# Four edits to a hybrid attention encoder: a joined product in band attention, later loads in the down projection, and a ring and two places around the output norms

## The chip, the core and the metric

The kernel runs on one core of a Trainium2 chip. The core has TensorE (PE in the profile, with its weight loads as PEld), VectorE (DVE), ScalarE (ACT), GpSimd (POOL) and SyncE (SP), which here issues the DMA transfers in the order of the program. Each engine has its own list of instructions in one order; semaphores tie the lists together. The metric is the device time of one execution in microseconds, lower is better.

## The reference, cut to what matters

One layer of an encoder, for a prompt of 2048 tokens and a sample of 32 tokens with 128 cached positions, width 1024, everything in float32:

```
z = rmsnorm(x) @ w_in                     # 1024 x 3072: q, k, v of two groups
oa = differential attention (4 heads, two maps of 64, values of 128), chunk-causal
ob = band attention (8 heads of 64), a 64-token chunk sees itself and 8 chunks before
     p = softmax(q k / 8 + bias, masked);  ob = p @ v
h  = x + concat(rmsnorm(oa), rmsnorm(ob)) @ w_out
h  = h + square(relu(rmsnorm(h) @ w_up)) @ w_down          # 4096 wide
h  = h + sigmoid(h @ w_ple_gate) * (p_in @ w_ple_proj)
y  = rmsnorm(h)                            # and the new keys and values are outputs
```

## The kernel before

Precision. The operands of the matmuls are in a reduced float32 form (fp32r in the profile's rows), so each operand is split in two: `hi`, a rounded copy (made on ACT or DVE), and `lo`, the rest (made on DVE or POOL). A product is then three matmuls: hi·hi, hi·lo, lo·hi. `mm3` (L254 and on) issues them, and `split` makes the parts.

Blocks. The tokens lie in four blocks of 512, 544, 512 and 512 columns (the sample rides in block 1). Tensors between the stages go through DRAM: `qS`, `kS`, `vS` (projections), `oT` (attention output), `hS` (the residual stream), `uS` (the MLP's hidden layer for blocks 2 and 3).

Stages. Norm and input projection per block (`prep`, `proj`); differential attention for the first half (`attn_a`); band attention (`attn_b`) for pairs of 128-token query tiles, interleaved with projections of later blocks and later with the output projection and the MLP of block 0; the output norm's sums (`onorm`), then `oload` (reads `oT`, scales, splits) and `outproj`; the MLP of blocks 0 and 1 by blocks (`mlp_up`, `mlp_down`); for blocks 2 and 3 together a seven-product scheme on half-size matrices (`uphase`, then `dphase`); the gates (`gate`, `gatepair`); the final norm.

Who sets the order. The Python code weaves generators into one another (`weave`, `weave2`), and the tile framework's scheduler then sets each engine's order by a simulated time line. A tile belongs to a ring of `bufs` buffers under a tag; a tile that is written again waits for the readers of the buffer's last content.

Band attention of one head and one pair of query tiles (`attn_b_pair`). Scores come in `sb` (PE), bias and row maximum on DVE, exponent and scaling on ACT. The weights are transposed on PE (`tpb`) and split: hi parts into `pH` (ACT), lo parts into `pL` (DVE), both tiles of six key tiles by 256 queries. Then per key tile two matmuls with the same stationary tile `vt` add into one PSUM tile `o` of 256 columns: one moves `pH`, one `pL`. The stationary tile has 128 columns: 64 of v's hi part, 64 of its lo part, so rows 0 to 63 of `o` hold v-hi times the weights and rows 64 to 127 v-lo times the weights. Where a key tile serves one query tile alone, the matmul has 128 columns. Last, ACT copies rows 64 to 127 to `t1`, and DVE adds rows 0 to 63. `o` has one buffer.

The down projection of blocks 2 and 3 (`dphase`). Seven products (numbers m = 3, 5, 7, 4, 2, 6, 1 in this order), each of eight steps c, each step of two k. For each k one `dx` (from `ut`, read from `uS`) and one `dw` (from one or two `wd`, read from `w_down`) are split, then 4 x 3 matmuls of 512 columns go to four PSUM tiles `dp`. `dx` has four buffers. At a product's end DVE adds `dp` into tiles of `h` (L1249). Product 3 adds into block 3 alone, product 5 into both blocks. Beside this PE works on the gates of blocks 0 and 1 (`gps`, `pps`), whose weights share the raw buffers with `ut`.

The ties (`hstep`, L1699). `h` of blocks 2 and 3 is read back from `hS` in 16 transfers of 256 KB. To keep them from starting early, each destination first gets one column copied from a `dx`; the transfer then has to wait for that copy.

Output projection. `oload(1)` is woven with `outproj(0)`, and the norm of block 0 (`norms(0)`, which runs `cnorm`) with `outproj(1)`. All take their scratch from the tag `tmp` of the pool `wk`, three buffers. `weave2(..., ONP)` places the steps of the output norms of blocks 0 and 1 between the steps of the last projections.

Of the kernel before, what the change touches and what calls it, by code (L numbers as in the profile page):

```python
# [12 lines left out]
F32 = mybir.dt.float32  # L13
F32R = mybir.dt.float32r
AF = mybir.ActivationFunctionType
ALU = mybir.AluOpType
# [3 lines left out]
P = 128  # L20
# [24 lines left out]
HALVES = [(0, 1), (2, 3)]  # L45
# [68 lines left out]
OW = 1  # L114
# [1 line left out]
JA0 = [(0, 1), (2, 3, 8)]  # L116
JA1 = [(4, 5), (6, 7)]
JB = [(0, 1), (2, 3, 8), (4, 5), (6, 7)]
ONP = (16, 1, 6)
ONQ = (8, 1, 1)  # L120
PW = 256
GL = 3
# [20 lines left out]
def weave(main, side, step, i=0, n=1):  # L143
    for _ in main:
        if i % step == 0:
            for _ in range(n):
                next(side, None)
        i += 1
    drain(side)
# [47 lines left out]
class Kern:  # L197
# [554 lines left out]
    def attn_b_pair(self, h, j, kt, v, kb, bb, q, ahead, pool, ps_s, ps_t, ps_o):  # L752
        nc = self.nc
# [4 lines left out]
        else:  # L758
            tiles, t0, nq = [2 * j, 2 * j + 1], tcol(256 * j), 256
        kfirst = 0 if samp else max(0, 2 * j - 4)  # L760
        pH = pool.tile([P, 6, 256], F32R, tag="pH", bufs=2, name="pHb")
        pL = pool.tile([P, 6, 256], F32R, tag="pL", bufs=2, name="pLb")
        spans = []
        for qi, t in enumerate(tiles):
            if samp:
# [30 lines left out]
            for x0 in range(0, len(kts), 4):  # L796
                ch = kts[x0 : x0 + 4]
                tp = ps_t.tile([P, 4, P], F32, tag="tp", name="tpb")
                for x, (i, kn) in enumerate(ch):
                    nc.tensor.transpose(  # L800
                        tp[:kn, x, :nr], e[:, P * (x0 + x) : P * (x0 + x) + kn], self.ident[:nr, :nr]
                    )
                groups = [(0, len(ch), P)] if not samp else [(0, 1, P), (1, 1, SS)]
                for a0, na, kn in groups:
                    sl = ch[0][0] - kfirst + a0
                    h_ = pH[:kn, sl : sl + na, P * qi : P * qi + nr]
                    l_ = pL[:kn, sl : sl + na, P * qi : P * qi + nr]
                    s_ = tp[:kn, a0 : a0 + na, :nr]
                    nc.scalar.activation(h_, s_, AF.Copy)
                    nc.vector.tensor_tensor(l_, s_, h_.bitcast(F32), op=ALU.subtract)  # L810
        ahead()
        o = ps_o.tile([P, 256], F32, tag="o", name="ob")
        order = []
        if samp:
            order = [(0, P, 0, nq), (1, SS, 0, nq)]
# [6 lines left out]
            order += [(i, P, 128, 256) for i in s1 if i not in s0]  # L822
        for x, (i, kn, qa, qb) in enumerate(order):
            vt = v[:kn, (SP - kb) // P + i] if samp else v[:kn, i - kb // P]
            for y, pt in enumerate((pH, pL)):
                nc.tensor.matmul(
                    o[:, qa:qb], vt, pt[:kn, i - kfirst, qa:qb],
                    start=x == 0 and y == 0, stop=x == len(order) - 1 and y == 1,
                )
        t1 = pool.tile([64, 256], F32, tag="t1", bufs=2, name="t1")[:, :nq]  # L830
        nc.scalar.activation(t1, o[64:128, :nq], AF.Copy)
        nc.vector.tensor_tensor(t1, o[0:64, :nq], t1, op=ALU.add)
        self.dma(self.oT[64 * m : 64 * m + 64, gi, t0 : t0 + nq], t1)

    def raw_o(self, wk, k, t0, n):
# [360 lines left out]
    def dphase(self, h, pool, md, step):  # L1196
# [32 lines left out]
        for m, sq, so, outs in plan:  # L1229
            ps = [md.tile([P, 512], F32, tag="mm", name="dp") for _ in range(4)]  # L1230
            for c in range(8):
                for k, (w, x) in enumerate(operands(m, sq, so, c)):
                    if m == 3 and k == 0:
                        step(c, x)
                    for d in range(4):
                        sl = slice(P * d, P * d + P)
                        self.mm3(
                            ps[d], [(w[:, 0, sl], w[:, 1, sl], x[:, 0], x[:, 1])],
                            start=c + k == 0, stop=c == 7 and k == 1,
                        )  # L1240
                if c < 7:
                    yield
            adds = [(d, q, op) for d in range(4) for q, op in outs]
            if m == 1:
                adds.sort(key=lambda x: x[1])
            for d, q, op in adds:
                i, t = int(q[0]) - 1, int(q[1]) - 1
                hv = h[2 + t][4 * i + d]
                nc.vector.tensor_tensor(hv, hv, ps[d], op=op)  # L1249
            yield  # L1250
# [231 lines left out]
    def run(self):  # L1482
        tc, nc, a = self.tc, self.nc, self.a
        with ExitStack() as top:
# [118 lines left out]
            def norms(b, act, ps):  # L1603
                r = self.colnorm(acc[b][0], b, 1.0 / D, wk, ps, "mm", None)
                yield
                yield from self.cnorm(b, wk, act, cn, r)

            acc = {b: [] for b in range(4)}
            with ExitStack() as x:
                oq = Sized(opened(x, "oq", 2), BLK, True)  # L1610
                weave(self.outproj(0, wk, oa[0], mm, acc[0]), self.oload(1, wk, oq, oa), 1, 0, OW)
                weave(self.outproj(1, wk, oa[1], mm, acc[1]), norms(0, actq, mm), 1, 1)
            hq = opened(sq_, "hq", 1)
            uq = Sized(opened(sq_, "uq", 10), BLK)
# [81 lines left out]
            h = {b: hh.tile([P, 8, 512], F32, tag="h", name="h") for b in HALVES[1]}  # L1696
            h = {b: [t[:, d] for d in range(8)] for b, t in h.items()}

            def hstep(c, x):  # L1699
                for b in HALVES[1] if c < 4 else ():  # L1700
                    for d in (2 * c, 2 * c + 1):
                        nc.gpsimd.tensor_copy(h[b][d][:, :1], x[:, 0, :1].bitcast(F32))
                    hmove(b, h[b], True, range(2 * c, 2 * c + 2))

            fk = opened(top, "fk", 1)
            udx, gqx = ExitStack(), ExitStack()
# [90 lines left out]
```

## Time and profile before

| | |
|---|---|
| median of 3 executions | 2965.36 us (2957.69 to 2965.66) |
| profiled execution | 2963.89 us |
| its span, first to last instruction | 2962.1 us |
| mean granted clock of TensorE | 0.993 |
| PE busy | 2899.6 us, 98% of the span |
| DVE, ACT, POOL busy | 1754.8, 1753.6, 1349.1 us |
| DMA | 578 MB, 195 GB/s on average |

A row of a group reads: line, engine, operation, tile written <- tiles read, shape, count | busy us, mean ns of one | idle time before it and what ended it. Durations of matmuls overlap, so the step between two starts tells what one costs. A row of the waits reads: who waited on whom: us in total, times, longest. A row of the time line reads: start us, us, engine, line, operation. A row of the windows gives the stretch, then the busy time and count of each engine, the granted clock, the DMA share and GB/s.

### The profile page before, as it was taken

The page shows a single profiled execution, that of the slowest core. Times are in us where ns is not written, and L with a number is a line of the kernel's source. Part 1 is how long each engine was busy: PE and PEld are TensorE (multiplying, and loading weights), DVE is VectorE, ACT ScalarE, POOL GpSimd, SP SyncE. Part 2 cuts the span into 40 slices and gives each one's busy share as a digit, 9 for nine tenths or more (in the row PEclk, how much of TensorE's full clock was granted, in tenths as well). Part 3 has the DMA queues.
Part 4 walks back from the last instruction along what each step waited for, and adds up shares of the span by engine and source line. Part 5 has one row for each costly group of instructions (what it writes and reads, how often), then busy time and mean ns, then how long its engine had stood idle before and what let it go on. Part 6 is the DMA issues. An engine that isn't in the chain of part 4 may idle for free.

```text
span 2962.1 us, 49251 instructions
## 1 busy us (share of the span) xinstructions
PE 2899.6 (98%) x17041; PEld 2560.4 (86%) x17041; DVE 1754.8 (59%) x3930; ACT 1753.6 (59%) x3729; POOL 1349.1 (46%) x1863
## 2 busy tenths in 40 slices
PE   8999999999999999999999999999999989999998
PEld 7899888998889888888899999889788868888886
DVE  6566664444565543565766564447665656766965
ACT  5566666665666665766777675443545445555554
POOL 4675664333355555655455455440855533133000
PEclk9999999999999999999999999999999999999999
DMA  9975578766677544544743433566443495756811
GB/s 347 328 249 198 192 259 271 219 210 207 226 252 225 192 159 157 166 154 151 240 138 123 148 109 120 183 205 199 164 149 139 146 342 191 267 194 202 265 64 57
DMA packets 299785, 578.28 MB, mean 195 GB/s; under 512 B 34672, under 2 KB 132080, under 8 KB 299536
## 3 DMA queue, kind: packets, MB, share of 16 engines
q1 hardware_dynamic: 299536, 575.13, 58.3%
q8 instruction: 135, 2.21, 0.3%
q14 instruction: 114, 0.93, 0.1%
HBM read 443.81 MB, written 131.22 MB: 194 GB/s over the span
## 4 chain that ended last, share of the span: by engine, by line
PE 89%; DMA 5%; DVE 3%; ACT 2%; issue 1%; POOL 1%; SPq 0%; ACTq 0%; DVEq 0%; POOLq 0%
PE s L607 4%; PE ups L269 4%; PE ups L267 4%; PE ups L268 4%; PE dps L267 4%; PE dps L268 4%; PE dps L269 4%; PE qps L267 4%; PE qps L269 4%; PE qps L268 4%; PE xps L269 3%; PE xps L268 3%; PE xps L267 3%; PE dp L267 3%; PE dp L269 3%; PE dp L268 3%
## 5 line engine op out<-in xcount | busy, mean ns | idle before, releaser
L230 POOL TENSOR_TENSOR wl<-wr,wh 128x256 fp32r<-128x256 f32 x888 | 667.8, 783 | 703.2 <-ACT wh L235 583.2
L235 ACT ACTIVATE wh<-wr 128x1024 fp32r<-128x1024 f32 x258 | 272.5, 1056 | 214.4 <-PE dps L268 43.5
L267 PE MATMUL ups<-cH,wh 128*128 128x272 f32 (+1 forms) x768 | 249.9, 326 | 2.3 <-ACT cH L235 1.2
L267 PE MATMUL dps<-uh,wh 128*128 128x272 f32 (+1 forms) x768 | 250.5, 328 | 1.5 <-DVE h L1001 1.1
L269 PE MATMUL ups<-cH,wl 128*128 128x272 f32 (+1 forms) x768 | 249.7, 326 | 0.6 <-DVE wl L241 0.6
L268 PE MATMUL ups<-cL,wh 128*128 128x272 f32 (+1 forms) x768 | 249.6, 325 | 0.0
L268 PE MATMUL dps<-ul,wh 128*128 128x272 f32 (+1 forms) x768 | 248.7, 324 | 0.2 <-DVE ul L241 0.2
L269 PE MATMUL dps<-uh,wl 128*128 128x272 f32 (+1 forms) x768 | 247.9, 324 | 0.0
L267 PE MATMUL qps<-aH,wh 128*128 128x512 f32 (+3 forms) x640 | 228.8, 357 | 6.6 <-DVE qk L487 3.0
L269 PE MATMUL qps<-aH,wl 128*128 128x512 f32 (+3 forms) x640 | 227.4, 355 | 0.0
L268 PE MATMUL qps<-aL,wh 128*128 128x512 f32 (+3 forms) x640 | 226.8, 354 | 0.0
L268 PE MATMUL dp<-dx,dw 128*128 128x512 f32 x448 | 177.9, 397 | 0.0
L267 PE MATMUL dp<-dx,dw 128*128 128x512 f32 x448 | 168.1, 399 | 9.1 <-ACT dx L235 9.1
L269 PE MATMUL dp<-dx,dw 128*128 128x512 f32 x448 | 174.9, 397 | 0.0
L607 PE MATMUL s<-ka,q 128*128 128x512 f32 (+3 forms) x640 | 173.3, 368 | 0.5 <-DVE nm L616 0.4
L788 DVE CUSTOM_DVE_ANT_0 eb<-sb,bb 128x320 f32<-128x320 f32 (+2 forms) x232 | 104.1, 478 | 109.3 <-PE tpb L800 105.0
L613 DVE TENSOR_REDUCE nm<-s 128x1 f32<-128x512 f32 (+1 forms) x192 | 122.1, 641 | 77.8 <-PE s L607 76.0
L267 PEld LDWEIGHTS ups<-cH,wh 128*128 128x128 f32 x768 | 145.2, 189 | 15.2 <-ACT cH L235 1.5
L267 PEld LDWEIGHTS dps<-uh,wh 128*128 128x128 f32 x768 | 144.6, 189 | 14.0 <-DVE h L1001 2.6
L269 PEld LDWEIGHTS ups<-cH,wl 128*128 128x128 f32 x768 | 145.0, 189 | 11.9 <-DVE wl L241 1.0
L268 PEld LDWEIGHTS ups<-cL,wh 128*128 128x128 f32 x768 | 145.3, 189 | 11.6 <-DVE cL L241 0.4
L268 PEld LDWEIGHTS dps<-ul,wh 128*128 128x128 f32 x768 | 144.8, 189 | 10.6 <-DVE ul L241 0.4
(278 smaller groups left out, 8949.4 us busy)
## 6 DMA issues: line engine op xcount, KB each, us to landing
wd<-w_down SPq DMA_DIRECT2D x96, 512.0 KB, 5.2
q<-qS SPq DMA_DIRECT2D x128, 256.0 KB, 4.2
v<-vSa SPq DMA_DIRECT2D x64, 512.0 KB, 3.6
wr<-w_up SPq DMA_DIRECT2D x64, 512.0 KB, 3.8
wr<-w_down SPq DMA_DIRECT2D x64, 512.0 KB, 3.8
ut<-uS SPq DMA_DIRECT2D x56, 512.0 KB, 4.3
wr<-w_qk SPq DMA_DIRECT2D x54, 512.0 KB, 5.2
kS<-qk SPq DMA_DIRECT2D x32, 512.0 KB, 5.4
```

Of the source, the lines that this page charges most:

```text
L230: nc.gpsimd.tensor_tensor(out[:, sl], a[:, sl], b[:, sl], op=op)
L235: nc.scalar.activation(hi, raw, AF.Copy)
L267: nc.tensor.matmul(ps, lh, rh, start=start and i == 0, stop=False)
L268: nc.tensor.matmul(ps, lh, rl, start=False, stop=False)
L269: nc.tensor.matmul(ps, ll, rh, start=False, stop=stop and i == n - 1)
L607: nc.tensor.matmul(s, q[:, m, hl, P * qi : P * qi + nr], kt[:, m, k0 - kb : k0 - kb + n], start=hl == 0, stop=hl == 1)
L613: nc.vector.tensor_reduce(nmx, s, axis=AX.X, op=ALU.max, negate=True)
L788: nc.vector.tensor_tensor_reduce(e[:, w * i : w * i + w], s, bb[:nr, b0 + w * i : b0 + w * i + w], 1.0, -3e38, ALU.add, ALU.max, st[:, 3 + ...
```

## The change

Four edits.

1. Band attention's two tiles `pH` and `pL` become one tile `pHL` with the parts side by side, and one matmul per key tile moves both: 2 x 256 columns, or 2 x 128 where a key tile serves one query tile. `o` has 512 columns in two halves, the product with the hi parts and that with the lo parts. At the end DVE adds rows 0 to 63 of both halves, one after the other; ACT copies rows 64 to 127 of the first half alone, so v-lo times the lo weights is left out of the sum now.
2. `hstep` is called in every product. The loads of block 3 are tied to steps 4 to 7 of product 3 (two each), those of block 2 to steps 0 to 7 of product 5 (one each). The tying copy is on ACT instead of POOL.
3. `oload(1)` and `cnorm` of block 0 take their scratch from a ring of their own, `ot`, of two buffers. As the pool is then a `Mix`, `oload` reads one tile ahead.
4. The output norms of blocks 0 and 1 move: their two steps stood at 16 and 22 (block 0) and 17 and 23 (block 1) of the projection's steps, and stand at 17 and 24, and at 23 and 30.

```
-ONP = (16, 1, 6)
+ONP = (17, 6, 7)
...
-        pH = pool.tile([P, 6, 256], F32R, tag="pH", bufs=2, name="pHb")
-        pL = pool.tile([P, 6, 256], F32R, tag="pL", bufs=2, name="pLb")
+        pHL = pool.tile([P, 6, 2, 256], F32R, tag="pHL", bufs=2, name="pHLb")
...
-                    h_ = pH[:kn, sl : sl + na, P * qi : P * qi + nr]
-                    l_ = pL[:kn, sl : sl + na, P * qi : P * qi + nr]
+                    h_ = pHL[:kn, sl : sl + na, 0, P * qi : P * qi + nr]
+                    l_ = pHL[:kn, sl : sl + na, 1, P * qi : P * qi + nr]
...
-        o = ps_o.tile([P, 256], F32, tag="o", name="ob")
+        o = ps_o.tile([P, 2, 256], F32, tag="o", name="ob")
...
-            for y, pt in enumerate((pH, pL)):
-                nc.tensor.matmul(
-                    o[:, qa:qb], vt, pt[:kn, i - kfirst, qa:qb],
-                    start=x == 0 and y == 0, stop=x == len(order) - 1 and y == 1,
-                )
+            nc.tensor.matmul(
+                o[:, :, qa:qb], vt, pHL[:kn, i - kfirst, :, qa:qb], start=x == 0, stop=x == len(order) - 1
+            )
         t1 = pool.tile([64, 256], F32, tag="t1", bufs=2, name="t1")[:, :nq]
-        nc.scalar.activation(t1, o[64:128, :nq], AF.Copy)
-        nc.vector.tensor_tensor(t1, o[0:64, :nq], t1, op=ALU.add)
+        nc.scalar.activation(t1, o[64:128, 0, :nq], AF.Copy)
+        for y in range(2):
+            nc.vector.tensor_tensor(t1, o[0:64, y, :nq], t1, op=ALU.add)
...
-                    if m == 3 and k == 0:
-                        step(c, x)
+                    if k == 0:
+                        step(m, c, x)
...
-                yield from self.cnorm(b, wk, act, cn, r)
+                yield from self.cnorm(b, wo, act, cn, r)
...
-                weave(self.outproj(0, wk, oa[0], mm, acc[0]), self.oload(1, wk, oq, oa), 1, 0, OW)
+                wo = Mix(wk, tmp=(opened(x, "ot", 1), 2))
+                weave(self.outproj(0, wk, oa[0], mm, acc[0]), self.oload(1, wo, oq, oa), 1, 0, OW)
...
-            def hstep(c, x):
-                for b in HALVES[1] if c < 4 else ():
-                    for d in (2 * c, 2 * c + 1):
-                        nc.gpsimd.tensor_copy(h[b][d][:, :1], x[:, 0, :1].bitcast(F32))
-                    hmove(b, h[b], True, range(2 * c, 2 * c + 2))
+            def hstep(m, c, x):
+                b, ds = {3: (3, range(2 * c - 8, 2 * c - 6) if c > 3 else ()), 5: (2, (c,))}.get(m, (2, ()))
+                for d in ds:
+                    nc.scalar.activation(h[b][d][:, :1], x[:, 0, :1].bitcast(F32), AF.Copy)
+                hmove(b, h[b], True, ds)
```

The scheduler's order moves with it. ACT at the start of `dphase` (`dx` and `dw` are the operands of the products, `hH` the split of the gate's `h`, `pT`, `pw`, `wh` the gate's other operands), before:

```order
L235 ACTIVATE dx<-ut 128x512
L235 ACTIVATE dw<-wd 128x512 x2
L235 ACTIVATE dx<-ut 128x512
L235 ACTIVATE dw<-wd 128x512
L235 ACTIVATE hH<-h 128x512 x8
L235 ACTIVATE dx<-ut 128x512 x2
L235 ACTIVATE pT<-pn 128x512
L235 ACTIVATE dx<-ut 128x512 x2
L235 ACTIVATE pT<-pn 128x512
L235 ACTIVATE dx<-ut 128x512
L235 ACTIVATE pw<-wr 128x512
L235 ACTIVATE wh<-wr 128x1024
```

and now:

```order
L235 ACTIVATE dx<-ut 128x512
L235 ACTIVATE dw<-wd 128x512
L235 ACTIVATE hH<-h 128x512 x8
L235 ACTIVATE dx<-ut 128x512 x2
L235 ACTIVATE pT<-pn 128x512 x2
L1701 ACTIVATE h<-dx 128x1 x4
L235 ACTIVATE pw<-wr 128x512
L235 ACTIVATE wh<-wr 128x1024
L235 ACTIVATE dw<-wd 128x512 x2
L235 ACTIVATE dx<-ut 128x512 x2
L1701 ACTIVATE h<-dx 128x1 x2
```

Seven `dx` stood ahead of `hH` in `dphase`, and ten stand there now; the tying copies are ACT's, after `hH`, a few at a time. On POOL the 16 copies, which stood right behind the `hL` pieces of that split, are gone.

SP at the same place (`wd`, `ut` as above, `h` of 8x512 the gate's, `h` of 128x512 the tied loads, `pn` and `wr` the gate's operands), before:

```order
L211 DMA pn<-pT 128x2x512
L211 DMA wd<-w_down 128x1024 x6
L211 DMA h<-hS 128x512 x16
L211 DMA wr<-w_ple_proj 128x2x256
L211 DMA wr<-w_ple_gate 128x1024
L211 DMA ut<-uS 128x1024
```

and now, from the gate's `w_ple_proj` on:

```order
L211 DMA wr<-w_ple_proj 128x2x256
L211 DMA wd<-w_down 128x1024
L211 DMA wr<-w_ple_gate 128x1024
L211 DMA wd<-w_down 128x1024 x3
L211 DMA ut<-uS 128x1024
L211 DMA wr<-w_ple_gate 128x1024
L211 DMA wd<-w_down 128x1024 x2
L211 DMA h<-hS 128x512 x4
L211 DMA ut<-uS 128x1024
L211 DMA wd<-w_down 128x1024
```

The first gate weights stood behind all 16 tied loads and stand ahead of them now. Ahead of these rows, from the first `wd` of `dphase` on, SP issues 12 `wd`, two `ut`, the gate's `h`, six stores to `uS` and `pn` in the new order. The tied loads go out in groups of four, two and one between the `ut` and `wd` of the following steps.

PE at a band product (`ob`) beside a projection of a later block, before:

```order
L826 MATMUL ob<-pHb,vbt 128x256
L826 MATMUL ob<-pLb,vbt 128x256
L826 MATMUL ob<-pHb,vbt 128x128
L826 MATMUL ob<-pLb,vbt 128x128
L800 MATMUL tpb<-ident,eb 128x128 x2
```

and now:

```order
L799 MATMUL tpb<-ident,eb 128x128 x3
L268 MATMUL vps<-wl,aH 128x256
L824 MATMUL ob<-pHLb,vbt 128x512 x3
L824 MATMUL ob<-pHLb,vbt 128x2x128
L799 MATMUL tpb<-ident,eb 128x128 x4
```

704 matmuls into `ob` become 352. Between 400 and 1200 us, where band attention is interleaved, the scheduler places most pieces anew.

## The prediction

> **What bounds the kernel now.** I read the busy shares first, then what TensorE (PE) waits for, then the stretch in which it waits most, in time order.
>
> ```profile
> PE 2899.6 (98%) x17041; PEld 2560.4 (86%) x17041; DVE 1754.8 (59%) x3930; ACT 1753.6 (59%) x3729; POOL 1349.1 (46%) x1863
> PE dp L267 <- ACT dx L235: 9.1, 2, 8.4
> PE gps L267 <- ACT wh L235: 3.8, 1, 3.8
> ```
>
> PE is busy for 98% of the span, so two things alone pay: fewer or shorter matmul slots, and PE's own waits. Of those (engine, line, awaited; total us, times, longest) the largest is `dp` on `dx`, 9.1 us, and the two quoted lie side by side in `dphase`. The columns of the next rows, cut by time, are length, busy time with count of PE, PEld, DVE, ACT, POOL, granted clock, DMA share, GB/s.
>
> ```profile
> 2384.00:2400.00 16.00, 16.00 (x70) 12.86 (x69) 13.63 (x23) 9.90 (x18) 0.00 (x0) 1.00 1.03 403
> 2405.20:2413.60 8.40, 0.12 (x1) 0.00 (x0) 7.40 (x7) 2.24 (x6) 8.40 (x17) 0.77 1.04 407
> 2409.60:2416.40 6.80, 2.69 (x6) 2.15 (x7) 5.52 (x7) 2.19 (x4) 6.77 (x19) 0.51 1.02 404
> 2429.00:2433.00 4.00, 0.34 (x2) 0.00 (x0) 0.00 (x0) 1.64 (x3) 1.41 (x2) 1.00 0.91 359
> 2433.40:2436.90 3.50, 3.50 (x10) 2.74 (x9) 3.30 (x4) 3.29 (x7) 3.50 (x4) 0.54 0.64 185
> 2440.00:2470.00 30.00, 30.00 (x131) 24.24 (x130) 20.37 (x33) 14.98 (x25) 6.74 (x9) 1.00 0.49 155
> ```
>
> PE stands still for 8.4 us and then 3.8 us, and each time the clock falls to about half for a while after. The DMA engines are full throughout; from 2440 on they are half idle. Why it stood still:
>
> ```profile
> 2384.49 0.39 PE L267 MATMUL dp<-dx,dw 128*128 128x512 f32 x1
> 2402.62 4.26 ACT L235 ACTIVATE hH<-h 128x512 fp32r<-128x512 f32 x8
> 2413.03 1.15 ACT L235 ACTIVATE dx<-ut 128x512 fp32r<-128x512 f32 x2 [6.16 <-POOL h L1702]
> 2403.31 8.75 POOL L220 TENSOR_TENSOR hL<-h,hH 128x256 fp32r<-128x256 f32 x8 [32.49 <-ACT hH L235]
> 2412.00 4.37 POOL L1702 COPY h<-dx 128x1 f32<-128x1 f32 x16
> 2413.53 11.35 SPq L211 DMA_DIRECT2D h<-hS  x16
> ```
>
> The first `dp` starts at 2384.5. The 16 tie copies (L1702) read the first `dx` of each of the steps 0 to 3, and stand on POOL behind 8.75 us of gate splits. Until they run, those buffers can't be written again; of the four that `dx` has, ever fewer turn over, and in the end ACT waits 6.16 us to make the next one. Then the 16 loads of `h` go out together, and the gate's first weights queue behind them, which is the second stall.
>
> **The ties (`hstep`).** The old ties go: none is left in steps 0 to 3, so four `dx` buffers turn over from the start. In ACT's new order ten `dx` stand ahead of `hH`, where seven did. PE's new order, like the old, has 144 `dp` before the first `gps`. What a 512-column matmul costs is the step between starts, here with six more between the two rows:
>
> ```profile
> 582.03 0.39 PE L268 MATMUL qps<-aL,wh 128*128 128x512 f32 x1
> 583.65 0.39 PE L269 MATMUL qps<-aH,wl 128*128 128x512 f32 x1
> ```
>
> 1.62/7 = 0.231 us. 144 of them from 2384.5 take 33.3 us, to 2418. The old order came to the `gps` at 2433, the end of the second stall.
>
> What goes away: waits of 9.1 and 3.8 us, and the half clock. In the two half-clock rows PE is busy for 2.69 and 3.50 us, at this step (five between the two rows):
>
> ```profile
> 2434.06 0.63 PE L268 MATMUL pps<-pT,pw 128*128 128x512 f32 x1
> 2436.20 0.63 PE L269 MATMUL gps<-hH,wl 128*128 128x512 f32 x1
> ```
>
> 2.14/5 = 0.43 instead of 0.23 loses 6.2 x (1 - 0.23/0.43) = 2.9 us. Together 15.8 us.
>
> What could stay. (a) The next `dx`: `hH` holds ACT for 4.26 us (2402.6 to 2406.9); four buffers at 12 matmuls each are 11 us of cover, enough. (b) The gate's weights: their load is no longer behind the 4 MB of `h`. The stretch moved
>
> ```profile
> DMA packets 10060, 25.73 MB, mean 343 GB/s; under 512 B 971, under 2 KB 1483, under 8 KB 10055
> wr<-w_ple_gate SPq DMA_DIRECT2D x3, 512.0 KB, 6.0
> ut<-uS SPq DMA_DIRECT2D x7, 512.0 KB, 4.6
> 2379.06 2.57 SPq L211 DMA_DIRECT2D wd<-w_down  x5
> ```
>
> in 2370 to 2445 (the last numbers of the middle rows are us from issue to landing). In SP's new order some 12.8 MB lie ahead of and with the first `w_ple_gate` (13 `wd`, two `ut`, the gate's `h` of 2 MB, six `uS`, `pn`, `w_ple_proj`): at 400 GB/s 32 us from 2379, so about 2411. Then comes POOL: by the row above a piece of a split takes 8.75/8 = 1.09 us there, `hL` ends at 2412, and two pieces of `pw` and four of the gate's `wl` stand behind it, so the last is ready at 2418.6 against the 2418 at which PE asks. I leave 2 us of the stall standing: the sum takes **-14**. Bounds: -15.8 (all gone), and -5 (DMA stays the limit and half of the 4.2 MB, worth 10.5 us at 400 GB/s, still lies in the stretch).
>
> What it adds: 16 one-column copies on ACT. The nearest row of such a size is
>
> ```profile
> L620 ACT ACTIVATION_READ_ACCUMULATOR e<-s,nm 128x1 f32 x192 | 38.7, 202 | 0.0
> ```
>
> 16 x 0.2 = 3.2 us, spread over two products in which ACT is half idle (14.98 of 30.00). Behind a copy on ACT wait the next splits of `dx` and `dw`; each copy reads what ACT has just written, so it doesn't wait itself. On SP an `h` load now stands between `ut` and `wd` loads; 16 x 256 KB into 2425 to 2550 is 8% more DMA share where 0.49 is in use. The adds into `h` need block 3 only at the end of the first product and block 2 from the end of the second, one step (24 matmuls, 5.6 us) or more after the last load was tied. Taken as 0; without that cover it is the last rival.
>
> **The band product.** Two products of 256 columns per key tile become one of 512 with the same stationary tile. One head and pair:
>
> ```profile
> 572.08 0.28 PE L826 MATMUL ob<-pLb,vbt 128*128 128x256 f32 x1
> 572.91 0.22 PE L826 MATMUL ob<-pHb,vbt 128*128 128x128 f32 x1
> 572.97 0.28 PE L826 MATMUL ob<-pLb,vbt 128*128 128x128 f32 x1
> ...
> 573.20 0.27 PE L826 MATMUL ob<-pLb,vbt 128*128 128x128 f32 x1
> 572.24 1.23 PE ob L826 x11
> ```
>
> Again the step between starts is the price. Seven wide ones fill 572.08 to 572.91, 0.119 each, and 128 columns take 0.11 to 0.12 too, except the first (0.06), whose weights had been loaded beside the wider matmul. So at 128 columns the weight load is the limit. Over eleven in a row, seven wide and four narrow: 1.23 - 7 x 0.119 = 0.397, or 0.099 for a narrow one. The counts, and in the last row the `ob` tile's own work (PE, PEld, DVE, ACT):
>
> ```profile
> L826 PE MATMUL ob<-pHb,vbt 128*128 128x256 f32 x224 | 59.6, 287 | 0.3 <-ACT pHb L809 0.3
> L826 PE MATMUL ob<-pHb,vbt 128*128 128x128 f32 x112 | 25.8, 247 | 0.0
> 420.00:1160.00 740.00, 107.44 (x704) 98.04 (x704) 27.74 (x72) 25.93 (x72) 1.00 0.66 213
> ```
>
> - 224 wide pairs: 2 x 0.119 become one of 0.231: 0.007 each, 1.6 us. Their second weight load was hidden, and saving it is worth nothing.
> - 112 narrow pairs: 2 x 0.099 become one of 256 columns at 0.119: 0.079 each, 8.9 us.
> - 16 sample pairs of 32 columns: 0.11 at most for a load saved; I take 0.8 us of the possible 1.7.
>
> Together **-11**, with bounds -15 (each narrow load at its full 0.11, all of the sample's) and -1.6 (only the wide pairs).
>
> By the Trainium skill, TensorE: Matmul & The Clock Gate, section "LDWEIGHTS (loading the stationary operand)", a load of 128 columns takes 128/1.2 = 107 ns, as the narrow steps show. Its section "Wait — 56ns, not 53.3ns?" has 55.6 ns between warm 128-column matmuls; were that the step here, the narrow pairs would save nothing. That is the second rival, and the steps above but the first speak against it.
>
> What it adds: each of the 72 adds on DVE a second time, 27.7 us.
>
> ```profile
> 430.00:1160.00 730.00, 721.91 (x4442) 642.04 (x4441) 360.45 (x1241) 470.23 (x975) 318.67 (x441) 1.00 0.66 211
> PE sb L785 <- DVE stb L788: 2.5, 3, 1.3
> 439.36 0.40 DVE L832 TENSOR_TENSOR t<-ob,t 64x256 f32<-64x256 f32 x1
> 440.57 0.37 PE L826 MATMUL ob<-pHb,vbt 128*128 128x256 f32 x1
> ```
>
> DVE is busy for 360 of the 730 us in which band attention runs beside the projections and the MLP; with the adds, 388. Behind the add wait the row maxima and the low parts of the next head; PE waited 2.5 us for such, three times. The one `o` buffer of PSUM comes free 0.4 us later; the last two rows are the closest of the 72 pairs, 0.8 us from the add's end to the next pair's first `ob`. I take 0; without cover it would be 27.7 us.
>
> **The ring and the norms' places.** `oload` and the first `cnorm` get two buffers of their own instead of sharing three. What PE lost there, in all:
>
> ```profile
> PE ups L267 <- ACT cH L235: 1.2, 1, 1.2
> PE ops L268 <- DVE oact L241: 1.0, 1, 1.0
> PE ops L267 <- DVE hd L901: 0.7, 2, 0.5
> 815.50:819.00 3.50, 3.47 (x9) 2.72 (x10) 3.50 (x4) 1.78 (x5) 2.84 (x3) 0.54 1.01 312
> ```
>
> 2.9 us of waits and 1.6 us of half clock (3.47 x (1 - 0.23/0.43)): 4.5 at most. I take **-1.5**. The new places of the two output norms (`ONP`) touch 6 of the 17041 matmuls, and no wait of PE is put down to them: 0, within 1 us. All of it, with the band, moves the scheduler's order from 400 to 1200 us; the waits quoted from there are of 0.5 to 1.3 us, and I allow 8 us either way.
>
> Here the row differs from a rule. The same page, Part 1, says that the clock halves after an idle window of about 3.4 us; at 815 it halved after a wait of 1.0. By the rule a 2 us rest of the stall would cost no clock, by the row another 1.6 us.
>
> **The sum.** The profiled execution took 2963.9 us (span 2962.1 and 1.8 around it), 1.5 below the median of three, 2965.4; those three spread over 8 us. 2963.9 - 14 - 11 - 1.5 = 2937.4. **I forecast 2937 us**, its own range 2929 to 2946.
>
> **The rivals.**
> - *The stretch is bound by transfers, not by the ties.* For it: a DMA share of 1.02 to 1.04 from 2384 on. Against: part of that was loads made early, and PE waited for `dx`, whose data had landed. The ties give -5: 2946.
> - *Narrow matmuls are not load-bound.* For it: the one step of 0.06. The band gives -1.6: 2947.
> - *The new order of 400 to 1200 us loses 8 to 10.* For it: each change of the order moves the short waits; against: none now is over 1.3 us. 2946.
> - *Slower: the tied loads hold up SP.* SP issues in order, and an `h` load that waits for ACT's copy holds back the `ut` and `wd` after it. There are 12 such steps (four of the first product, eight of the second). It decides from the point at which a `ut`, issued after the tie, lands (4.6 us) and is split on ACT and DVE (1.2 us, twice the 1.15/2 of ACT's row) later than the four `dx` buffers last, 11 us; if each step then lost 3 us, 36 us: 2937 + 36 = 2973. Against: that needs a wait of 5 us on SP at each.
> - *The change does less than it says*: none of its edits is without instructions in the new order, so this is left with the first two.
>
> **Chances.** Forecast 0.58; transfers 0.14; not load-bound 0.08; order 0.13; slower 0.04; the rest, 0.03, is a gain beyond 2925. The first four, two of them joined, reach to 2954, so the range is 2925 to 2954. 0.3%, about what a measurement can tell from no change, is 9 us: faster means under 2956. Of the rivals only two at once come near it: faster 0.88, same 0.08, slower 0.04.
>
> **What would show it.** In the new profile: no wait of `dp` on `dx` over 1 us, the first `gps` at about 2418 on the old time scale, no half clock there; 352 `ob` matmuls, narrow pairs at a step of 0.12, DVE 28 us busier. The prediction is wrong if PE still stands still after the last `dx` ahead of `hH`, if `ob` runs of six (four wide, two narrow) take over 1.25 us, or if new waits on DVE appear between 430 and 1160.

## The result, and the profile after

The changed kernel takes 2941.1 us (median of 4 runs, 2938.4 to 2942.6), the kernel before 2963.2 us beside it (4 runs, 2957.7 to 2965.7). The ratio is 0.9927, with a 95% interval of 0.9911 to 0.9942: 22 us less, 17 to 26 by the interval. The profiled execution took 2942.6 us with a span of 2940.8. The forecast was 2937.

The first rows answer to those that the prediction opened with: the busy shares, and the largest waits of PE that the change brought or left (engine, line, awaited; total us, times, longest).

```profile
PE 2882.5 (98%) x16689; PEld 2533.0 (86%) x16689; DVE 1775.8 (60%) x4002; ACT 1758.5 (60%) x3745; POOL 1351.8 (46%) x1847
```

```profile
PE s L607 <- ACT e L620: 5.8, 5, 2.7
PE sb L784 <- DVE stb L787: 3.5, 5, 1.6
PE ops L267 <- DVE hd L899: 2.8, 2, 1.9
PE ops L267 <- ACT oact L235: 2.0, 3, 1.3
```

The waits of `dp` on `dx` (9.1 us) and of `gps` on `wh` (3.8 us) are gone. A wait that the kernel before did not have stands first among these now: `s`, the scores of the differential attention, on `e`.

The start of `dphase`, cut by time as in the prediction (length, busy time and count of PE, PEld, DVE, ACT, POOL, granted clock, DMA share, GB/s):

```profile
2380.00:2413.40 33.40, 33.40 (x145) 26.86 (x144) 30.11 (x41) 21.89 (x42) 12.91 (x12) 1.00 1.03 405
2413.40:2450.00 36.60, 36.60 (x159) 29.61 (x158) 24.36 (x37) 19.09 (x38) 15.37 (x19) 1.00 0.81 295
```

PE never stands still, and the clock is full. The DMA engines are as full as before until 2413, so their load had not been the bound. From the first `dp` to the first `gps` it is 33.7 us now and was 48.6; the prediction had 33.3.

The joined product, shape by shape (busy us, mean ns of one | idle time before):

```profile
L824 PE MATMUL ob<-pHLb,vbt 128*128 128x512 f32 x224 | 62.8, 396 | 0.0
L824 PE MATMUL ob<-pHLb,vbt 128*128 128x256 f32 x112 | 27.2, 286 | 0.0
```

With 16 more of 64 columns these are the 352 foretold. What they cost is the step from each start to the next start on PE, summed over all: 69.9 us, and 84.4 us before. By shape, before and after: wide 57.3 and 52.4, narrow 22.5 and 14.6, sample 4.6 and 2.9.

So 14.5 us went out of the band product, and 16.6 out of the start of `dphase` and what follows it, 31 together; 21 arrived. Where the rest went is seen by stages. Each row of the table adds up to the span; the stages end with the last `ob` (band attention), the last `o` (second differential attention), the first `xps` (up phase), the first `dp`, the first `gps`.

| us | to last `ob` | to last `o` | to first `xps` | to first `dp` | to first `gps` | to the end | sum |
|---|---|---|---|---|---|---|---|
| before | 1154.6 | 674.2 | 240.0 | 315.7 | 48.6 | 529.0 | 2962.1 |
| after | 1166.3 | 661.5 | 236.5 | 315.6 | 33.7 | 527.2 | 2940.8 |

The last three stages give 16.8 us, the first three only 4.4. The band ends **11.8 us later**, though its product is 14.5 us shorter. The attention behind it is 12.7 us shorter, which just gives that back: it ends at 1827.8, where it ended at 1828.8.

The first three stages as rows, before:

```profile
430.00:1154.60 724.60, 716.51 (x4419) 637.61 (x4417) 360.04 (x1240) 468.58 (x972) 314.69 (x435) 1.00 0.66 212
1154.60:1828.90 674.30, 671.40 (x4352) 617.68 (x4350) 410.67 (x872) 468.46 (x1081) 371.09 (x539) 1.00 0.47 155
1828.90:2068.50 239.60, 236.81 (x1530) 217.82 (x1529) 125.13 (x196) 101.39 (x169) 77.59 (x104) 0.99 0.60 192
```

and after:

```profile
430.00:1166.40 736.40, 730.19 (x4200) 637.06 (x4199) 387.33 (x1313) 481.86 (x987) 338.28 (x464) 1.00 0.66 212
1166.40:1828.00 661.60, 652.23 (x4292) 602.33 (x4291) 402.08 (x870) 461.45 (x1069) 353.70 (x514) 0.99 0.47 155
1828.00:2064.10 236.10, 228.40 (x1448) 206.90 (x1447) 124.81 (x195) 97.38 (x163) 71.23 (x92) 0.99 0.59 191
```

In the second stage PE lacked 2.9 us of being always busy (674.30 - 671.40) and lacks 9.4 now; in the third 2.8, and 7.7 now. In the band PE is as full as it was. There the freed time was filled with products of the MLP (`ups` and `dps`): 626 of them stood ahead of the last `ob`, 768 stand there now. The 142 more are block 0's, of 512 columns, and by their steps they take 33.4 us there. So the band's later end is more work done early, and in itself no loss. But these products are missing later: behind the band the MLP's steps are 33.8 us less, and the two stages there are shorter by 16.2 us alone. The other 17.6 were lost in them: 11.4 as idle PE, the two rises just named, and the rest in longer steps. PE's time line in the tail of the second attention:

```profile
1785.69 0.73 PE L607 MATMUL s<-ka,q 128*128 128x512 f32 x2 [0.72 <-ACT e L620]
1789.16 0.73 PE L607 MATMUL s<-ka,q 128*128 128x512 f32 x2 [1.59 <-ACT e L620]
1790.88 1.12 PE L682 MATMUL tpp<-ident,e 128*128 128x128 f32 x4 [0.99 <-DVE e L646]
1794.74 2.07 PE L607 MATMUL s<-ka,q 128*128 128x512 f32 x4 [2.75 <-ACT e L620]
1796.62 0.43 PE L267 MATMUL dps<-uh,wh 128*128 128x272 f32 x1
```

From 1772.3 to 1796.6 there is no product of the MLP, and PE waits for the attention's own chain. The clock goes with it (the window's columns are as above):

```profile
1790.00:1800.20 10.20, 6.57 (x24) 5.75 (x25) 7.50 (x18) 6.47 (x17) 3.22 (x4) 0.51 0.04 14
```

In the kernel before PE was busy for 49.95 of the 50 us from 1750 to 1800. Two questions follow. Is this tail the place where the band's gain was lost? And why does so much of the MLP come ahead of the band's end?

### The profile page after: what moved, and what is told of

Read it like the earlier page. It is cut to its first block, busy times and chain, and to the rows that moved or that the text cites. A ratio compares the mean times of both kernels' runs of the same rounds, so it can differ in the third digit from the quotient of the medians.

```text
span 2940.8 us, 48636 instructions
## 1 busy us (share of the span) xinstructions
PE 2882.5 (98%) x16689; PEld 2533.0 (86%) x16689; DVE 1775.8 (60%) x4002; ACT 1758.5 (60%) x3745; POOL 1351.8 (46%) x1847
## 4 chain that ended last, share of the span: by engine, by line
PE 92%; DMA 2%; DVE 2%; ACT 1%; issue 1%; POOL 0%; SPq 0%; ACTq 0%; DVEq 0%; POOLq 0%
PE s L607 4%; PE dps L267 4%; PE dps L269 4%; PE dps L268 4%; PE ups L269 4%; PE ups L268 4%; PE ups L267 4%; PE qps L267 4%; PE qps L269 4%; PE qps L268 4%; PE dp L267 4%; PE dp L268 4%; PE dp L269 4%; PE xps L268 3%; PE xps L269 3%; PE xps L267 3%
## 5 line engine op out<-in xcount | busy, mean ns | idle before, releaser
L230 POOL TENSOR_TENSOR wl<-wr,wh 128x256 fp32r<-128x256 f32 x888 | 671.9, 787 | 695.0 <-ACT wh L235 574.9
L235 ACT ACTIVATE wh<-wr 128x1024 fp32r<-128x1024 f32 x258 | 272.4, 1056 | 212.8 <-PE dps L268 39.6
L620 ACT ACTIVATE e<-s,nm 128x512 f32<-128x512 f32 (+1 forms) x192 | 124.3, 652 | 51.7 <-DVE nm L613 33.0
L269 PEld LDWEIGHTS ups<-cH,wl 128*128 128x128 f32 x768 | 144.5, 188 | 11.8 <-DVE wl L241 1.2
```

The source lines that it names most:

```text
L230: nc.gpsimd.tensor_tensor(out[:, sl], a[:, sl], b[:, sl], op=op)
L235: nc.scalar.activation(hi, raw, AF.Copy)
L269: nc.tensor.matmul(ps, ll, rh, start=False, stop=stop and i == n - 1)
L620: nc.scalar.activation(dst, src, AF.Exp, bias=nmx, scale=1.0 if near is None else -1.0, accum_out=z[:nr, m, bi : bi + 1],)
```

## Experiments: the parts one by one

All times are beside runs of the kernel before on the same chip, as a ratio to it with its 95% interval.

**The ties alone**, on the kernel before; the edit is the part of the change's diff on `step` and `hstep`.

> The kernel before with the later ties alone: the tied hidden rows are those of the projection's last step and are copied by ScalarE; band product and ring as before. Theory (the two stalls ahead of the first gate product came from the ties, and they are worth the 16.5 us of idle and half-clock time that went between 2400 and 2450): the waits of 8.4 and 3.8 us are gone, the first scaled-gate product comes about 34 us after the first down product instead of 48.6, and the time falls by 14 to 17 us to 2946 to 2950. Rival (transfers bound that stretch, so that a stall comes back elsewhere): a fall of 5 us, to about 2958. If the whole gain of 22 us came from the ties, 2941.

Measured: 2944.2 us, 0.9945 (0.9931 to 0.996), 14 us less by the medians and 16 by the ratio; the first `gps` comes 33.7 us after the first `dp`, and neither wait is left. The theory's number holds, and the transfers did not bound the stretch.

**The band product alone**, on the kernel before; the edit is the part on `pHL`, `ob` and the second add.

> The kernel before with the one-tile weight parts alone (one output product per key tile, the second addition on VectorE, the instance-long output tile); ties and ring as before. Theory: the output products' slots shrink by about 14 us in the stretch, but the MLP of block 1 then runs out of work before the second attention ends, so that only 4 to 6 us arrive at the end: 2957 to 2959, with waits of `s` and `o` on ScalarE and VectorE in the last 50 us of that attention. Rival (the slots' 14 us arrive, and the loss in the tail belongs to the ring or to the ties): 2949 to 2952. Second rival (VectorE's 28 us of additions eat the gain all along the stretch): no change, 2961 to 2965, with the waits spread over the band and not at its tail.

Measured: 2954.2 us, 0.9985 (0.9975 to 0.9994), 4.4 us less, as the theory has it. The `ob` steps shrink to 71.2 us in all, by 13.3, and 9 of these are lost again. Its profile has a wait of `s` on `e` of 2.3 us at 1792.8.

**The change without its ties.**

```
-            def hstep(m, c, x):
...
+            def hstep(c, x):
+                for b in HALVES[1] if c < 4 else ():
+                    for d in (2 * c, 2 * c + 1):
+                        nc.gpsimd.tensor_copy(h[b][d][:, :1], x[:, 0, :1].bitcast(F32))
+                    hmove(b, h[b], True, range(2 * c, 2 * c + 2))
```

> The changed kernel with the early ties on GpSimd put back. Theory: the two stalls return, 14 to 17 us slower than the changed kernel, 2955 to 2958. Rival (the later ties also moved something in the band): a loss above 20 us, as good as the kernel before, 2962. Rival (transfers bound): a loss of 5 us, 2946.

Measured: 2956.5 us, 0.9995 (0.9986 to 1.0005). The wait is back as it was:

```profile
PE dp L267 <- ACT dx L235: 9.1, 2, 8.4
```

Against the changed kernel (0.9927, and 0.9936 when it was run again) that is 17 to 20 us. By its own spans it is 14.9 (2955.7 against 2940.8), so the ties are worth 15 to 20 us here and 14 to 16 alone, and the rest of the change arrives as little or nothing.

**The change again, and without the own ring.**

```
-                yield from self.cnorm(b, wo, act, cn, r)
+                yield from self.cnorm(b, wk, act, cn, r)
...
-                wo = Mix(wk, tmp=(opened(x, "ot", 1), 2))
-                weave(self.outproj(0, wk, oa[0], mm, acc[0]), self.oload(1, wo, oq, oa), 1, 0, OW)
+                weave(self.outproj(0, wk, oa[0], mm, acc[0]), self.oload(1, wk, oq, oa), 1, 0, OW)
```

> The changed kernel, unaltered, beside the three that follow, so that they are compared on one chip. Expected: 0.992 to 0.9945 of the kernel before, 17 to 23 us less.

> The changed kernel without the own ring: the copies of the first block's norm share the ring of the other small tiles again, as before. Theory (from the traces of the single parts: with the band product alone the up phase's first product stands at 2058.1 us, with the ring beside it at 2062 to 2064, so the ring costs in the middle): 3 to 5 us faster than the changed kernel. Rival (the prediction's step: the ring takes away a wait of 1.5 us): 1 to 3 us slower. Rival (those differences are the scatter of single profiles): within 1.5 us of it.

Measured: 2939.9 us, 0.9936 (0.9923 to 0.9948), and without the ring 2939.4 us, 0.994 (0.9928 to 0.9953). The ring is worth nothing that can be told. My theory that it costs 3 to 5 us came from single profiles and falls; its third reading, scatter, stands.

## Experiments: what held the `dx` buffers

The prediction had the early ties wait on POOL behind 8.75 us of splits. So they were put on ACT at the early places:

```
-                b, ds = {3: (3, range(2 * c - 8, 2 * c - 6) if c > 3 else ()), 5: (2, (c,))}.get(m, (2, ()))
-                for d in ds:
-                    nc.scalar.activation(h[b][d][:, :1], x[:, 0, :1].bitcast(F32), AF.Copy)
-                hmove(b, h[b], True, ds)
+                ds = range(2 * c, 2 * c + 2) if m == 3 and c < 4 else ()
+                for b in HALVES[1]:
+                    for d in ds:
+                        nc.scalar.activation(h[b][d][:, :1], x[:, 0, :1].bitcast(F32), AF.Copy)
+                    hmove(b, h[b], True, ds)
```

> The changed kernel with the tied rows copied at the early places again (projection step 3, first four chunks), but by ScalarE as in the change and not by GpSimd. It tells the engine of the copy from its place. Theory (both matter: the 8.4-us stall came from GpSimd's queue holding the partial sums' buffers and goes; the 3.8-us stall came from 4 MB of hidden rows that are loaded ahead of the gate weights and stays): 4 to 7 us slower than the changed kernel. Rival (the place alone matters): all 15 us are lost. Rival (the engine alone matters): within 1.5 us of it.

Measured: 2957.0 us, 0.9998 (0.9989 to 1.0007): all of it is lost, as the rival for the place alone says. Its waits:

```profile
PE dp L267 <- ACT dx L235: 7.7, 2, 6.9
...
PE gps L267 <- ACT wh L235: 3.7, 1, 3.7
```

and ACT's time line between the last `dx` ahead of the copies and the first behind them:

```profile
2393.16 0.63 ACT L235 ACTIVATE dx<-ut 128x512 fp32r<-128x512 f32 x1 [2.18 <-PE dp L269]
2393.69 0.62 ACT L235 ACTIVATE dw<-wd 128x512 fp32r<-128x512 f32 x1
2394.22 4.26 ACT L235 ACTIVATE hH<-h 128x512 fp32r<-128x512 f32 x8
2401.68 1.60 ACT L1702 ACTIVATE h<-dx 128x1 f32<-128x1 f32 x16 [3.21 <-DMA pn<-pT]
2403.19 1.66 ACT L235 ACTIVATE dx<-ut 128x512 fp32r<-128x512 f32 x3
```

The copies stand behind the gate's split on ACT too, and then wait 3.21 us more, until a transfer has landed. Only after them is a `dx` made again. They begin 25.6 us after the first `dp` (2376.1 in this run); on POOL, before, it was 27.5 (2412.0 - 2384.5). So POOL's queue is some 2 us of it: ACT was free for the copies 3.21 us earlier and they could not run, and a `dx` that they read can't be written again until they have. The changed kernel's own ties show what may be the reason (first and last start, then what their engine sat idle for):

```profile
L1701 ACT ACTIVATE h<-dx x16: 184/187/204, 2407.3 to 2499.1; 128x1 f32<-128x1 f32 x16
...
DMA uS<-u: 2.8, 1
```

They too wait, 2.8 us, for a transfer: a store of the up phase into `uS`. The tiles of `h` are opened after those of the up phase have been closed, so I take it that they lie in the same memory and that the tie has to wait for the last store out of it. The row of the early ties names another transfer (`pn`), but that run's issues speak for the stores too (time line of SP; then KB each and us from issue to landing):

```profile
2395.02 0.32 SPq L211 DMA_DIRECT2D uS<-u  x1
2396.25 0.58 SPq L211 DMA_DIRECT2D pn<-pT  x1
uS<-u SPq DMA_DIRECT2D x1, 256.0 KB, 6.6
pn<-pT SPq DMA_DIRECT2D x1, 512.0 KB, 6.7
```

The last store landed at 2401.6, 0.1 us ahead of the first copy (2401.68). `pn` landed at 2402.9, when the copies were running, so they did not wait for it. That the early ties wait for the stores is thus in the trace; that shared memory is the reason is argued from the program, not shown.

**The late places, but on POOL.**

```
-                    nc.scalar.activation(h[b][d][:, :1], x[:, 0, :1].bitcast(F32), AF.Copy)
+                    nc.gpsimd.tensor_copy(h[b][d][:, :1], x[:, 0, :1].bitcast(F32))
```

> The changed kernel with the tied rows copied at the late places, but by GpSimd. With the early places on ScalarE the stall was as long as on GpSimd; here the other half. Theory (the place alone decides): within 2 us of the changed kernel, 0.992 to 0.995 of the kernel before. Rival (GpSimd's queue is too late for a copy at any place, since it works through the gate's splits): a wait of `dp` on `dx` is back and 5 us or more are lost.

Measured: 2941.0 us, 0.9938 (0.9924 to 0.9952), the same as the changed kernel, with no wait of `dp` on `dx`. The place decides, and the engine does not.

## Experiments: where the band's gain went

**The switch one chunk later.** From chunk 9 of 16 on, block 1's MLP may take PSUM buffers from the attention's ring `s` also.

```
-                        if ch == 9 and part == 0:
+                        if ch == 10 and part == 0:
```

> The changed kernel with one number moved: block 1's MLP goes over to taking its PSUM buffers from the attention's ring at chunk 10 instead of chunk 9. Theory (the band's freed time is lost at the tail of the second attention because the MLP has reached the switch and offers TensorE nothing more to do there): the waits of 0.5 to 2.8 us between 1770 and 1800 and the half clock behind them go or shrink, and the time falls by 6 to 10 us to 2931 to 2935. Rival (the tail is bound by the attention's own chain of ScalarE and VectorE, whatever lies beside it): the attention ends at the same time, the MLP's work is done a little earlier, the time falls by 0 to 3 us. Rival (the switch was where it was for a reason: the products collide over PSUM): slower by 3 to 10 us.

Measured: 2936.6 us, 0.9921 (0.9905 to 0.9938). From the changed kernel's 0.9927 and 0.9936 that can't be told apart, but the profile says where the time went (windows, columns as above; then a wait):

```profile
1750.00:1800.00 50.00, 50.00 (x381) 48.88 (x380) 33.96 (x72) 34.87 (x85) 23.46 (x34) 1.00 0.33 104
1800.00:1870.00 70.00, 55.46 (x324) 48.06 (x324) 33.18 (x55) 35.22 (x68) 26.50 (x36) 0.90 0.46 151
```

```profile
PE ops L267 <- ACT oact L235: 9.4, 3, 8.9
```

The waits up to 1800 are gone: 381 matmuls where the changed kernel has 275. In their place PE waits 8.9 us at 1842 for `oact`, the input of the second half's output projection. That projection is handed out between the pieces of the same MLP (the number of its pieces per part of a chunk stands in the table `SIDE`), and it stood now right behind the attention's last product.

**The switch and that side work one chunk later.**

```
-SIDE = {**{i: (2, 2, 1) for i in range(9, 14)}, 14: (2, 1, 1), 15: (2, 1, 1)}
+SIDE = {i: (2, 2, 2) for i in range(10, 16)}
...
-                        if ch == 9 and part == 0:
+                        if ch == 10 and part == 0:
```

> The changed kernel with the switch of the PSUM ring at chunk 10, and also the side work (the output projection of the second half) handed out from chunk 10 on, two pieces at each part. Theory (with the switch alone the waits in the attention's tail went, but 9 us of waiting for the side work's input appeared at 1842, because it stood ahead of the MLP's filler; handed out one chunk later it finds its input ready): 3 to 8 us faster than the changed kernel, and no wait above 3 us between 1770 and 1870. Rival (the second attention's own chain ends at 1825 to 1830 in every trace and what is left behind it is fixed): within 1.5 us of it.

Measured: 2930.9 us, 0.9911 (0.9897 to 0.9924), on one chip with the changed kernel's 2939.9: 9 us faster, one more than expected. The second half of the expectation failed, for a wait stayed, and a longer one:

```profile
1841.87 0.39 PE L708 MATMUL ss<-sl,ones_r 128*128 128x256 f32 x1 [0.19 <-POOL sl L220]
1852.51 0.79 PE L267 MATMUL ops<-oact,wh 128*128 128x512 f32 x1 [10.25 <-ACT oact L235]
```

The gain came all the same: 176 more `ups` and `dps` stand ahead of the last `o` than in the changed kernel, and so many fewer behind it.

**The same on the kernel before**, to see whether the later order is better in itself.

> The kernel before, with the later switch of the PSUM ring and the later side work that took 9 us off the changed kernel, and nothing else. It tells whether those 9 us are the band's gain that the changed kernel had lost in the attention's tail. Theory (they are: before, TensorE's work lasted to the end of the second attention anyway, the waits of over 0.5 us there add up to less than 2 us, so there is little to win): 0 to 3 us faster than the kernel before, or somewhat slower. Rival (the later switch is simply a better order, band or no band): 7 to 10 us faster than the kernel before, and the band's gain went elsewhere.

Measured: 2955.7 us, 0.9987 (0.9978 to 0.9995), 2.9 us less by the medians. The same edit is worth 9 us with the change (2939.9 to 2930.9) and 3 us without. Most of it is thus time that the band product had freed and the tail had lost.

**Both at chunk 11.**

```
-SIDE = {**{i: (2, 2, 1) for i in range(9, 14)}, 14: (2, 1, 1), 15: (2, 1, 1)}
+SIDE = {i: (3, 2, 2) for i in range(11, 16)}
...
-                        if ch == 9 and part == 0:
+                        if ch == 11 and part == 0:
```

> The changed kernel with switch and side work at chunk 11 (three, two, ... pieces a part). With both at chunk 10 a wait of 10.2 us for the side work's input was left at 1852, because the output projection stood directly behind the attention's last product; here 11 down products of the MLP and more stand between them. Theory: that wait shrinks below 3 us and the time falls by another 4 to 9 us, to 0.988 to 0.990 of the kernel before. Rival (the side work is now too late, and the PSUM ring too short for it): within 2 us of the version at chunk 10, or slower.

Measured: **2921.2 us**, 0.9874 (0.9861 to 0.9888), 37 us below the kernel before, faster than both kernels of this case and a little below the 0.988 to 0.990 expected. Whether the side work alone, without the switch, would do as much was not tried. PE's busy time and count, granted clock, DMA share and GB/s from 1750 to 1870, here

```profile
1750.00:1800.00 50.00, 50.00 (x382) 1.00 0.33 104
1800.00:1870.00 70.00, 68.67 (x496) 1.00 0.45 145
```

and in the changed kernel

```profile
1750.00:1800.00 50.00, 42.36 (x275) 0.90 0.24 75
1800.00:1870.00 70.00, 63.57 (x409) 0.97 0.47 155
```

The wait for `oact` is down to 0.2 us on ScalarE, since 20 us of the MLP's products stand between the attention's last one (1835.4) and the output projection's first (1855.5). Its first three stages:

```profile
430.00:1163.50 733.50, 729.24 (x4201) 635.64 (x4201) 386.91 (x1313) 481.78 (x987) 339.69 (x464) 1.00 0.66 212
1163.50:1835.50 672.00, 670.05 (x4477) 622.75 (x4475) 413.12 (x885) 471.45 (x1093) 347.91 (x508) 1.00 0.47 156
1835.50:2039.60 204.10, 201.82 (x1264) 182.60 (x1262) 109.12 (x175) 85.61 (x137) 76.56 (x98) 1.00 0.62 206
```

The second attention ends 7.5 us later than in the changed kernel, and the up phase begins 24.5 us earlier: 185 fewer products of the MLP are left in between (872 against 1057), at 0.13 us each 24 us. The up phase then takes 319.1 us, 3.5 more than in the changed kernel, so some of the gain is lost again there.

**Without the second addition.**

```
-        for y in range(2):
-            nc.vector.tensor_tensor(t1, o[0:64, y, :nq], t1, op=ALU.add)
+        nc.vector.tensor_tensor(t1, o[0:64, 0, :nq], t1, op=ALU.add)
```

> The changed kernel without the second addition of each output product on VectorE: the low parts of the weights are left out of the output, 72 additions of about 0.38 us, 27 us of VectorE's time less. Theory (VectorE has room, and the added work is not what ate the band's gain): within 2 us of the changed kernel. Rival (the additions lie on the path through the next head's maxima): 5 us or more faster.

Measured: 2928.1 us, 0.9896 (0.9882 to 0.9909): against 0.9927 to 0.9936 for the changed kernel that is 9 to 12 us, the two profiled spans lie 11.9 us apart, and the intervals (0.9882 to 0.9909, and 0.9911 to 0.9942 or 0.9923 to 0.9948) don't meet. The rival wins, and the theory on which I had taken the additions for free falls. Its first three stages:

```profile
430.00:1155.10 725.10, 720.31 (x4169) 629.54 (x4168) 361.67 (x1243) 477.69 (x986) 335.56 (x462) 1.00 0.66 214
1155.10:1815.80 660.70, 657.41 (x4329) 608.48 (x4328) 408.48 (x873) 460.19 (x1072) 362.02 (x519) 1.00 0.47 157
1815.80:2052.10 236.30, 228.01 (x1447) 206.43 (x1446) 125.60 (x195) 97.03 (x163) 71.78 (x92) 0.99 0.58 191
```

The band ends at 1155.0, as before the change, and everything behind it lies 11 to 12 us earlier than in the changed kernel. The second attention takes 660.7 us, with 37 more products of the MLP in it than the changed kernel has in its 661.6.

Put beside each other (in us, from the traces; MLP: `ups` and `dps`):

| | MLP ahead of last `ob` | last `ob` | second attention | its idle PE | MLP left behind it | first `xps` |
|---|---|---|---|---|---|---|
| before | 626 | 1154.6 | 674.2 | 2.9 | 1140 | 2068.8 |
| after | 768 | 1166.3 | 661.5 | 9.4 | 1057 | 2064.3 |
| one addition | 732 | 1155.0 | 660.6 | 3.3 | 1056 | 2052.4 |
| chunk 11 | 768 | 1163.4 | 671.9 | 2.0 | 872 | 2039.8 |

## Why the prediction was right, and where not

*The ties, -14.* Right in kind, a little small. The stretch gave 16.6 us (14.9 up to the first `gps`, 1.7 behind it, where the second half clock had been), above the upper bound of 15.8 that I had set. The 2 us of the stall that I left standing did not stay. The reason given was half right: the ties did hold `dx`, but all but some 2 us of that had nothing to do with POOL: on ScalarE, at the same early places, the gain was lost as well.

*The band product, -11.* It gave 14.5 in its own steps. The narrow pairs gave 8.0 for 8.9, the sample's 1.7 for 0.8, the wide pairs 4.9 for 1.6. I had priced a wide pair by the step inside a run of seven; over all pairs, with the beginnings and ends of the runs, two products took 0.256 (57.3/224) and not 0.238, one takes 0.234.

*The addition on DVE, "I take 0".* This step failed. Its cost is 9 to 12 us, a third or more of its 27.7 us. I had looked for it in PE's waits in the band (2.5 us on DVE before, 3.5 now) and at DVE's load (360 of 725 us), and neither shows it. It shows in the order: with two additions 36 more `dps` of 512 columns stand ahead of the band's last `ob` than with one (768 products against 732), and by their steps these take 8.8 us. The `ob` steps are longer by 1.1 us and PE's idle time there by 1.4. Together that is about the 11.3 us by which the band ends later. With one addition the 36 stand in the second attention instead. It is no longer for that (660.6 against 661.5 us), as they fill 6.1 us of PE's waits there, and its tail has no half clock. So most of the price looks to be the loss in the tail, and not a second one beside it.

How the addition moves the order stays open in part: taking it away changes both DVE's work and the order that the scheduler reckons from it. The run without the ring has two additions and, as with one, 732 products ahead; there PE has 8.7 us more idle time up to the last `ob` than with one addition, much of it on `hd` and `oact`. So another order pays in waits. Whether the addition costs anything when switch and side work stand at chunk 11 was not run.

A later end of the band would cost nothing if what PE did meanwhile were saved later. Much of it was not, for the second attention seems to have a chain of its own: it takes 660.7 us (one addition) and 661.6 (two) with PE idle for 3.3 and for 9.4 us, and no run here has it below 659. PE's work freed there turns into waits unless the MLP has pieces left to offer at that point. The changed kernel had none between 1772 and 1796. With switch and side work at chunk 11 it has, and the time comes out.

*The ring, -1.5.* Not seen: 0.9936 with it, 0.994 without.

*The order's 8 us either way.* This is where the loss came to stand, and the third rival (the new order loses 8 to 10) had its price, though not its place: it looked at 400 to 1200, and the waits stand at 1776 to 1796 and 1845 to 1860. The rivals on transfers and on narrow products fall with the runs of single parts and the steps. The slower one falls as well: the tied loads cost nothing.

So the sum was 2963.9 - 14 - 11 - 1.5, and the runs have it as 2963.9 - 16.6 - 4.4, with 0.2 from the up phase: 2942.7, where the profiled execution took 2942.6. The forecast came within 4 us of the median since a tie term too small stood against a middle term too large (12.5 for 4.4). The ties' term was reasoned; that it ran over and made up for part of the middle's 8 us was luck.

## What to carry to other kernels

Time freed on a full engine arrives only if that engine has work to do wherever the next chain of latencies begins: after such an edit, look at the next stage's tail for waits, and move the filler (here by the switch's chunk and one table, worth another 16 to 18 us). An engine at half load is not a free place for an added instruction in a chain of heads; price it by leaving it out once, not by the waits of the engine that one watches. And a copy that ties a transfer to a point in the program holds its source until it can run; here, at the early places, the hold was nearly as long on ScalarE as on GpSimd.

## What was not expected of the hardware

The half clock in the tail lasted 10.2 us (1790.0 to 1800.2, granted clock 0.51), three times the usual 3.4, after waits of which none ahead of it was over 1.6 us; inside it PE waited once for 2.75 us and was busy for 6.57 us. Cut in three:

```profile
1790.30:1793.70 3.40, 1.12 (x4) 0.72 (x4) 3.40 (x5) 2.05 (x4) 2.94 (x3) 0.50 0.01 2
1793.70:1797.10 3.40, 2.35 (x7) 1.93 (x8) 2.12 (x6) 2.48 (x7) 0.00 (x0) 0.50 0.12 39
1797.10:1800.50 3.40, 3.40 (x17) 3.40 (x17) 1.88 (x9) 1.70 (x7) 0.00 (x0) 0.50 0.00 0
```

PE was busy for 1.12, 2.35 and 3.40 us of the three, and the full clock came back behind the full one. By the Trainium skill, TensorE: Matmul & The Clock Gate, Part 1, the clock is given back after a busy window of about 3.4 us; the trace agrees with that. The same section's idle window of about 3.4 us ahead of the halving does not fit the trace: the waits of 0.72, 0.17 and 1.59 us between 1785 and 1790 add up to 2.5 us and were enough. In the last 3.4 us ahead of the halving PE was still busy for 1.40 us. In the kernel before, too, it was busy for 1.80, 1.78, 1.06 and 1.74 us of the 3.4 ahead of the half clocks at 815.8, 887.4, 1426.8 and 1843.2. So the wait of 1.0 us that the prediction names at 815 was not alone in its window. At what busy share the clock falls was not measured.

The DMA engines were at a share of 1.03 for 33 us at the start of `dphase` (405 GB/s) without PE waiting at all. A full queue there was no sign of a bound.
